# Down projection, every second load: the second part of a weight made by a negated copy and an adding transfer

## The chip, the cores and the metric

The kernel runs on one core of a Trainium2 chip. The core has a matrix engine (TensorE, PE in the profile; its weight loads are a track of their own, PEld), three engines for elementwise work (VectorE, DVE; ScalarE, ACT; GpSimd, POOL), SyncE (SP), which here only issues transfers, and 16 DMA engines that carry every transfer, whichever engine's queue issued it. The engines run side by side and wait for each other through semaphores; each works through its own instructions in order.

The metric is the device time of one execution in microseconds, the median over several runs. The profile is one execution taken with the hardware profiler on, and its times are counted from the start of its span.

## The reference, cut to what matters

A two-layer encoder on 256 tokens of width 1024. Each layer has a token mixer (pooling branch, dilated attention branch, gates, output projection) and then a gated MLP with a width-3 convolution over the tokens. The change lies in the MLP:

```python
a, gval = jnp.split(xn @ w_up, 2, axis=-1)          # w_up: 1024 x 5632
a = lax.conv_general_dilated(a, conv_w[:, None, :], ...) + conv_b
return (jax.nn.gelu(a) * gval) @ w_down             # w_down: 2816 x 1024
...
h = h + _conv_ffn(...)                              # last, a final RMSNorm
```

All inputs and outputs are float32.

## The kernel before, in words

**Numbers in two parts.** TensorE works on a rounded 32-bit format. To keep the precision of float32, an operand is split: the first part is the number rounded to that format, the second is the number less the first part. A product then takes three matmuls: first by first, first by second, second by first. `row_mm` (L582 to L587) does so in the down projection: L585 multiplies the activation's first part with the weight's first part (`wh`), L586 the activation's first part with the weight's second part (`wl`), L587 the activation's second part with `wh`.

**Weights.** `Weights` (L97) feeds all of them. `add` notes a load of 1 MB, which is cut into two pieces of 128x1024 numbers (512 KB); `use` puts the pieces on a list in the order in which TensorE will want them. `load` (L127) issues the transfer from DRAM on SyncE's queue into one of three `raw` buffers. `open_next` (L179) splits a piece: ScalarE casts `raw` into `wh` (L201), and VectorE subtracts `wh` from `raw` into `wl` (L203). There are five buffers for `wh` and five for `wl` (`BUFS`). `get` (L224) hands a piece to the code that multiplies with it, and first sees to it that the three pieces behind it (`LOOK`) are split.

**The MLP.** It goes over 22 blocks f of 128 hidden channels, two at a time (L1331). `up(f)` (L1262) computes a block of the up projection (`proj`, L551; matmuls on L543 with tile `proj_ps`), adds up its sums (L579, L580), does the convolution (L1274 on ScalarE, L1275 and L1278 on VectorE), the GELU (L1288 and L1292 on ScalarE, L1289 and L1293 on VectorE), the gate (L1297 or L1303), and splits the result (L1308, L1309). From f = 6 on, two steps of the down projection follow each pair of blocks. They use the activations of six blocks earlier (`LAG`), and each step multiplies with one piece of `w_down`: four sums (two sets of tokens by two halves of the columns), three matmuls each, tile `res_ps`. The last four pieces are held and multiplied at the end, sum by sum. At f = 4, 8, 12 and 14 half of a group of the gate's values is computed as well (`t_ps`, L667).

The list of pieces is written in the same order ahead of time (L310 to L322): for each second f the columns of `w_up`, then, from f = 6 on, two pieces of `w_down`, and at the end the pieces that are left.

**Order.** The order of each engine's instructions is made when the program is built, by a scheduler that goes by the order in which the code issues them and by its own estimate of when each is ready. It may move an instruction past others of its engine; at run time nothing is reordered.

Of the kernel before, what the change touches and what calls it, by code (L numbers as in the profile page):

```python
# [13 lines left out]
ALU = mybir.AluOpType  # L14
# [82 lines left out]
class Weights:  # L97
# [8 lines left out]
    def __init__(self, tc, pool, idle):  # L106
        self.tc, self.nc, self.pool, self.idle = tc, tc.nc, pool, idle
        self.loads, self.pieces = [], []
        self.n_loaded, self.n_split, self.n_got = 0, 0, 0
        self.raw, self.split = {}, {}  # L110
        self.live = set()
        self.behind, self.later = (), []
        self.last = [None, None]
        self.loads_behind = {}
        self.n_scaled, self.gains = 0, None

    def add(self, src, shape, cuts, tag=None):

        n = len(self.loads)
        self.loads.append((src, shape, tag))  # L120
        return [(n, cut, c_shape) for cut, c_shape in cuts]
# [57 lines left out]
    def open_next(self):  # L179


        nc, i = self.nc, self.n_split
        n, cut, shape, slot = self.pieces[i]
        if slot is None:
            self.live.add(i)
            h, l = (
                self.pool.tile([P, *shape], F32R, tag=tag, bufs=self.BUFS, name=f"{tag}{i}")
                for tag in ("wh", "wl")
            )
        else:  # L190
            tag, part, of = (*slot, 0, 1)[:3]
            if part == 0:
                self.shared = self.idle.tile([P, of, 2, *shape], F32R, tag=tag, name=f"{tag}{i}")
            h, l = self.shared[:, part, 0], self.shared[:, part, 1]
        src = cut(self.raw[n])
        self.split[i] = (h, l)
        self.n_split += 1
        if i >= self.n_scaled:
            def make(n):
                if n == 0:  # L200
                    inst = nc.scalar.copy(out=h, in_=src)  # L201
                else:
                    inst = nc.vector.tensor_sub(out=l, in0=src, in1=h.bitcast(F32))  # L203
                self.last[n] = inst
                return inst

            return [(lambda: make(0), lambda: make(1))]

        def scaled(j):
            k = (i * shape[0] + j) % KD  # L210
            g = self.gains[:, k : k + 1]
            return (
                lambda: nc.scalar.activation(h[:, j], src[:, j], AF.Copy, scale=g),
                lambda: nc.vector.scalar_tensor_tensor(
                    out=l[:, j], in0=src[:, j], scalar=g, in1=h[:, j].bitcast(F32),
                    op0=ALU.mult, op1=ALU.subtract,
                ),

                lambda: nc.vector.tensor_scalar_mul(h[:, j], src[:, j], g),
            )  # L220

        return [scaled(j) for j in range(shape[0])]
# [19 lines left out]
def encoder(ctx, tc, x, w_in, w_pool, pool_scale, w_a, w_b, w_o, norm1, norm2, w_up, conv_w,  # L242
            conv_b, w_down, rel_bias, norm_f, onehot, edges, out):
    nc = tc.nc
# [9 lines left out]
    W = Weights(tc, wpool, big)  # L254

    def cols(w, c0):

        src = w[:, c0 : c0 + 256].rearrange("(k p) c -> p k c", p=P)
        return W.add(
            src, (8, 256), [((lambda t, j=j: t[:, :, j * P : (j + 1) * P]), (8, P)) for j in (0, 1)]  # L260
        )

    def rows(w, r0, n=2, c0=0, width=1024, tag=None, pieces=2):

        src = w[r0 : r0 + n * P, c0 : c0 + width].rearrange("(k p) c -> p k c", p=P)
        h = n // pieces
        return W.add(
            src, (n, width), [((lambda t, j=j: t[:, j * h : (j + 1) * h, :]), (h, width)) for j in range(pieces)],
            tag,
        )  # L270

    first_up = []
    for l in range(DEPTH):
        for g in range(NG):
            c0 = C_V + g * 512
            slots = (("m2", 0, 2), ("m2", 1, 2), ("ybig",), ("at2",)) if g == 0 else ()
            for j in range(2):
                tag = "k1" if l == 0 and g == 1 and j == 0 else None
                W.use(rows(w_in[l], j * 512, 4, c0, 512, tag), slots[2 * j : 2 * j + 2])
        if l == 0:  # L280
            W.n_scaled = len(W.pieces)
        for c in range(3, -1, -1):
            W.use(cols(w_in[l], c * 256))
        for n, c in enumerate(PAIRS):
            pool = ([], [])
            if n == 1:
                pool = W.add(
                    w_pool[l].rearrange("g (k p) c -> p (g k) c", p=P), (8, 256),
                    [((lambda t, j=j: t[:, 4 * j : 4 * j + 4, :]), (4, 256)) for j in range(2)],
                )  # L290
                pool = (pool[:1], pool[1:])
            W.use(pool[0] + cols(w_in[l], C_Q + c * 256))
            W.use(pool[1] + cols(w_in[l], C_K + c * 256))
        for w, c0 in ((w_a[l], 0), (w_in[l], C_GP)):
            for c in (c0, c0 + 512):
                W.use(rows(w, 0, 4, c, 512) + rows(w, 512, 4, c, 512))
        for c in (0, 512):
            W.use(rows(w_in[l], 0, 4, C_GA + c, 512) + rows(w_in[l], 512, 4, C_GA + c, 512))
            W.use(rows(w_b[l], 0, 4, c, 512))
        for c in range(4):  # L300
            W.use(rows(w_o[l], c * 256))
        first_up.append((len(W.pieces), len(W.loads)))
        slots = (("v1",), ("ybig",), ("at2",))
        for j in range(2):
            tag = None if j else "k1"
            W.use(rows(w_up[l], j * 512, 4, 0, 512, tag), slots[2 * j : 2 * j + 2])
        for n in range(3):
            for j in range(2):
                W.use(rows(w_up[l], j * 512, 4, DFF + n * 512, 512))
        for f in range(4, NF, 2):  # L310
            if f in HALF_GROUPS:
                n, j = HALF_GROUPS[f]
                W.use(rows(w_up[l], j * 512, 4, DFF + n * 512, 512))
            a = cols(w_up[l], f * P)
            if f >= 4 * NQ:
                g = cols(w_up[l], DFF + f * P)
                a = [a[0], g[0], a[1], g[1]]
            W.use(a)
            if f >= LAG:
                W.use(rows(w_down[l], (f - LAG) * P))  # L320
        for f in range(NF - LAG, NF, 2):
            W.use(rows(w_down[l], f * P))  # L322
# [228 lines left out]
    def proj(x2, n=1):  # L551


        if not ready:
            pieces = [W.get() for _ in range(n)]
            ps = [mmp.tile([P, 2, S], F32, tag="mm", name="proj_ps") for _ in range(n)]
            two_sums(
                x2, KD,
                *(
                    (b, lambda k, wh=wh: wh[:, k, :], lambda k, wl=wl: wl[:, k, :])  # L560
                    for b, (_, (wh, wl)) in zip(ps, pieces)
                ),
            )
            for i, _ in pieces:
                W.free(i)
            ready.extend((b[:, 0], b[:, 1]) for b in ps)
        return ready.pop(0)

    def halves(a):

        return a.rearrange("p (t m) -> p t m", t=2)
# [331 lines left out]
    for l in range(DEPTH):  # L903
# [49 lines left out]
        for gi in range(3, -1, -1):  # L953
# [10 lines left out]
            cur, n = u, S + 2 * PAD  # L964
            sh = 1
            while sh < w:
# [3 lines left out]
                    out=nxt[:, :, 0:n], in0=cur[:, :, 0:n], in1=cur[:, :, sh : sh + n]  # L970
# [7 lines left out]
            if hw > 1:  # L978
# [5 lines left out]
                out=pd, in0=cur[:, :, o : o + S], scalar=1.0 / w, in1=u[:, :, PAD : PAD + S],  # L984
# [130 lines left out]
        for m, c in enumerate(PAIRS):  # L1115
# [7 lines left out]
            for n in range(4):  # L1123
                if m == 1:
                    next(pool_parts)
                src, rest = (halves(a) for a in proj(x2, 1 + (m != 1)))
                hd = 2 * c + n % 2
                scale = HD**-0.5 if n < 2 else 1.0
                if hd < HPG:
# [3 lines left out]
                        out=lo[:, hd], in0=src, scalar=scale, in1=hi[:, hd].bitcast(F32),  # L1133
# [3 lines left out]
                        out=lo[:, hd], in0=rest, scalar=scale, in1=lo[:, hd].bitcast(F32),  # L1137
                        op0=ALU.mult, op1=ALU.add,
                    )
                else:  # L1140
# [3 lines left out]
                        out=o, in0=src, scalar=scale, in1=o, op0=ALU.mult, op1=ALU.add  # L1144
# [18 lines left out]
        for cc in HALVES:  # L1163
# [4 lines left out]
            for t in range(2):  # L1168
                nc.vector.scalar_tensor_tensor(
                    out=pa[:, t, cc], in0=th[:, t], scalar=1.0, in1=pa[:, t, cc],  # L1170
# [4 lines left out]
        piece, load = first_up[l]  # L1175
        made = None
        for n, cc in enumerate(HALVES):
# [5 lines left out]
            for t in range(2):  # L1183

                with tc.issue_after((turned if t else made[1]).ins) if n + t else ExitStack():
                    nc.vector.scalar_tensor_tensor(
                        out=th[:, t], in0=th[:, t], scalar=1.0, in1=ps[t], op0=ALU.add, op1=ALU.mult
# [187 lines left out]
```

## Time and profile before

| | |
|---|---|
| Median of 3 runs | 859.94 us (859.87 to 860.45) |
| Profiled execution, span | 858.0 us |
| TensorE busy | 851.6 us (99%) |
| VectorE busy | 661.2 us (77%) |
| ScalarE busy | 493.8 us (58%) |
| GpSimd busy | 32.0 us (4%) |
| Moved by DMA | 186.81 MB, 218 GB/s on average |

The profiled execution has its span as its only time: from the first to the last instruction of the program. The timed runs also count what lies around the span. A row of the profile names the line of the kernel, the engine, the operation and the tiles (out<-in), the shape and the number of instructions; behind the bar stand the busy time, the mean time of one in nanoseconds, and the idle time of the engine ahead of them with what ended it. A row of the timeline has the start, the time taken, and in square brackets the idle time of the engine ahead of it. Matmuls overlap in TensorE's pipeline: a row of 0.39 us for a 128x512 matmul starts 0.23 us behind the one before.

### The profile page before, as it was taken

To read this page: it belongs to the slowest core of one execution; us is meant where nothing else is said; L and a number is where in the kernel's file an instruction comes from. 1 tells how busy PE (TensorE), PEld (TensorE's weight loads), DVE (VectorE), ACT (ScalarE), POOL (GpSimd) and SP (SyncE) were. 2 spreads that over 40 slices of the span, in tenths; PEclk is the share of its full clock that TensorE was granted. 3 is DMA by queue.
4 is the path that set the end of the run, shared out by engine and by line. 5 is a ranking of instruction groups with operands and counts; after the bars stand their busy time and mean duration, and the time that the engine had idled before them with its cause. 6 is when DMAs were issued, how large, how long until landed. Compare 5 with 4: busy or idle time off the path is not lost.

```text
span 858.0 us, 11823 instructions
## 1 busy us (share of the span) xinstructions
PE 851.6 (99%) x4343; PEld 727.9 (85%) x4343; DVE 661.2 (77%) x1050; ACT 493.8 (58%) x795; POOL 32.0 (4%) x98
## 2 busy tenths in 40 slices
PE   9999999999999999999999999999999999999997
PEld 8888888888888888888888889988888888888886
DVE  7998796667767788888855987874776777988894
ACT  7756654455445476666645665543654555775672
POOL 1710000000010000000000000000000000000001
PEclk9999999999999999999999999999999999999999
DMA  9686547766747876666736555658667478676641
GB/s 331 217 248 206 196 163 231 240 228 229 250 182 246 270 249 231 231 235 206 245 99 209 184 199 192 198 175 268 226 243 275 154 249 259 246 256 208 239 147 49
DMA packets 136387, 186.81 MB, mean 218 GB/s; under 512 B 5561, under 2 KB 88193, under 8 KB 136329
## 3 DMA queue, kind: packets, MB, share of 16 engines
q1 hardware_dynamic: 136168, 185.79, 63.8%
q8 instruction: 34, 0.56, 0.3%
q10 hardware_dynamic: 160, 0.27, 0.1%
q14 instruction: 25, 0.20, 0.1%
HBM read 172.39 MB, written 13.65 MB: 217 GB/s over the span
## 4 chain that ended last, share of the span: by engine, by line
PE 99%; DVE 0%; ACT 0%; POOL 0%; issue 0%; POOLq 0%; ACTq 0%
PE proj_ps L543 34%; PE t_ps L667 30%; PE v_ps L667 6%; PE res_ps L586 6%; PE res_ps L585 6%; PE res_ps L587 6%; PE v_ps L895 3%; PE v_ps L802 1%; PE pool_ps L543 1%; PE o_ps L1086 1%; PE s_ps L1034 1%; PE s_ps L1029 1%; PE o_ps L1082 1%; PE xt_ps L481 1%; PE gain_ps L372 0%; PE xt_ps L750 0%
## 5 line engine op out<-in xcount | busy, mean ns | idle before, releaser
L203 DVE TENSOR_TENSOR wl<-raw,wh 128x1024 fp32r<-128x1024 f32 x274 | 329.8, 1217 | 88.1 <-ACT wh L201 73.6
L201 ACT CAST wh<-raw 128x1024 fp32r<-128x1024 f32 x274 | 284.3, 1049 | 118.3 <-PE t_ps L667 49.0
L543 PE MATMUL proj_ps<-x,wh 128*128 128x512 f32 x832 | 196.9, 390 | 0.0
L543 PEld LDWEIGHTS proj_ps<-x,wh 128*128 128x128 f32 x832 | 154.3, 188 | 30.9
L667 PE MATMUL t_ps<-wh,x 128*128 128x512 f32 x576 | 179.7, 390 | 0.0
L667 PEld LDWEIGHTS t_ps<-wh,x 128*128 128x128 f32 x576 | 107.8, 188 | 22.3
L667 PE MATMUL t_ps<-wl,x 128*128 128x512 f32 x288 | 112.1, 389 | 0.0
L543 PEld LDWEIGHTS proj_ps<-x,wl 128*128 128x128 f32 x832 | 105.4, 191 | 3.0
L543 PE MATMUL proj_ps<-x,wl 128*128 128x256 f32 x832 | 107.8, 283 | 0.0
L586 PE MATMUL res_ps<-wl,actq 128*128 128x512 f32 (+1 forms) x184 | 70.0, 380 | 0.0
L587 PE MATMUL res_ps<-wh,actk 128*128 128x512 f32 (+1 forms) x184 | 69.9, 380 | 0.0
L585 PE MATMUL res_ps<-wh,actq 128*128 128x512 f32 (+1 forms) x184 | 69.7, 381 | 0.0
L667 PEld LDWEIGHTS t_ps<-wl,x 128*128 128x128 f32 x288 | 54.1, 188 | 11.2
L667 PE MATMUL t_ps<-wh,po 128*128 128x512 f32 x128 | 41.4, 395 | 0.0
L587 PEld LDWEIGHTS res_ps<-wh,actk 128*128 128x128 f32 x184 | 34.6, 188 | 6.6
L586 PEld LDWEIGHTS res_ps<-wl,actq 128*128 128x128 f32 x184 | 34.6, 188 | 6.4
L585 PEld LDWEIGHTS res_ps<-wh,actq 128*128 128x128 f32 x184 | 34.5, 188 | 6.3
L454 POOL TENSOR_SCALAR ss<-ss 128x1 f32<-128x1 f32 x8 | 2.0, 253 | 779.6 <-ACT junk L447 779.6
L1308 ACT CAST actq<-g 128x256 fp32r<-128x256 f32 x44 | 17.0, 403 | 20.7 <-DVE g L1297 20.0
L667 PEld LDWEIGHTS t_ps<-wh,po 128*128 128x128 f32 x128 | 24.0, 188 | 4.9
L447 ACT ACTIVATE junk<-h 128x512 f32<-128x512 f32 (+1 forms) x19 | 10.5, 553 | 28.6 <-DVE h L445 28.5
L579 ACT COPY a<-proj_ps 128x256 f32<-128x256 f32 x36 | 13.6, 389 | 23.3 <-PE proj_ps L543 23.3
(204 smaller groups left out, 1148.9 us busy)
## 6 DMA issues: line engine op xcount, KB each, us to landing
raw<-in_w_in_dram SPq DMA_DIRECT2D x58, 1024.0 KB, 5.4
raw<-in_w_up_dram SPq DMA_DIRECT2D x44, 1024.0 KB, 6.9
raw<-in_w_down_dram SPq DMA_DIRECT2D x22, 1024.0 KB, 4.7
raw<-in_w_a_dram SPq DMA_DIRECT2D x8, 1024.0 KB
raw<-in_w_o_dram SPq DMA_DIRECT2D x8, 1024.0 KB, 7.1
crossing<-crossing SPq DMA_DIRECT2D x12, 512.0 KB, 5.4
turning<-turning SPq DMA_DIRECT2D x8, 512.0 KB, 2.8
turned_p<-turning SPq DMA_DIRECT2D x32, 128.0 KB, 3.3
```

The costliest lines, as they stand in the source:

```text
L201: inst = nc.scalar.copy(out=h, in_=src)
L203: inst = nc.vector.tensor_sub(out=l, in0=src, in1=h.bitcast(F32))
L447: nc.scalar.activation(junk[:, 0 : cc.stop - cc.start], h[:, t, cc], AF.Square, scale=D**-0.5, accum_out=ss[:, n : n + 1],)
L481: nc.tensor.transpose(pt[:, k, :], xn[:, c0 : c0 + P], ident)
L543: nc.tensor.matmul(out, w(k), x, start=(steps is first and k == 0), stop=(steps is last and k == nk - 1), skip_group_check=turns["rest"],)
L579: nc.scalar.copy(out=out, in_=sums[1])
L585: nc.tensor.matmul(ps, ah, wh, start=first, stop=False, skip_group_check=on)
L586: nc.tensor.matmul(ps, ah, wl, start=False, stop=False, skip_group_check=on)
L587: nc.tensor.matmul(ps, al, wh, start=False, stop=last, skip_group_check=on)
L667: nc.tensor.matmul(ps, x2[:, 2 * n + j, part, t, :], w[:, j, :], start=(n + m == 0), stop=(n == last and m == 5),)
L895: nc.tensor.matmul(ps[t], a[:, k, t, :], w[:, j, :], start=(k + m == 0), stop=(k == KD - 1 and m == 2),)
L1308: nc.scalar.copy(out=ah, in_=g)
```

## The change

At f = 6, 10, 14 and 18 the two pieces of `w_down` put on the list are marked (`by_dma`). For a marked piece the second part is made in another way. ScalarE still casts `raw` into `wh`. Then ScalarE writes minus `raw` into `wl`, which is rounded on the way, so that `wl` holds minus the first part. Then a transfer on GpSimd's queue reads the same rows of `w_down` from DRAM a second time and adds them onto `wl`, which leaves the weight less its first part. VectorE's subtraction falls away for these pieces. The loads at the other f, and the six pieces behind f = 20, are as before.

```diff
@@ class Weights, __init__
         self.n_scaled, self.gains = 0, None
+        self.by_dma = set()
@@ class Weights, open_next
-        src = cut(self.raw[n])
+        load, src = n, cut(self.raw[n])
...
             def make(n):
                 if n == 0:
                     inst = nc.scalar.copy(out=h, in_=src)
+                elif i in self.by_dma:
+                    nc.scalar.mul(out=l, in_=src, mul=-1.0)
+                    nc.gpsimd.dma_start(out=l, in_=cut(self.loads[load][0]), accum_op=ALU.add)
+                    return None
                 else:
                     inst = nc.vector.tensor_sub(out=l, in0=src, in1=h.bitcast(F32))
@@ encoder, the list of pieces
             if f >= LAG:
+                if f % 4 == 2:
+                    W.by_dma |= {len(W.pieces), len(W.pieces) + 1}
                 W.use(rows(w_down[l], (f - LAG) * P))
```

`self.loads[load][0]` is the part of `w_down` in DRAM from which the raw buffer was loaded, and `cut` takes the piece's half of it.

## The prediction

> **What bounds the kernel now.** I read the page first, then the busy time by stretches, then the rows of ScalarE and TensorE around the loads that the change names.
>
> ```profile
> span 858.0 us, 11823 instructions
> PE 851.6 (99%) x4343; PEld 727.9 (85%) x4343; DVE 661.2 (77%) x1050; ACT 493.8 (58%) x795; POOL 32.0 (4%) x98
> ```
>
> The span is 858.0 us, and the median of the three runs is 859.94: 1.9 us lie around the span, and I add every difference to 859.94. TensorE is busy for all but 6.4 us. The chain of waits agrees (PE 99%), so a microsecond counts only where TensorE waits for it. The change works in the gated MLP; the first stretch below lies in that of the first layer, the second in that of the second, and the last holds the end. Busy time of each engine by stretch (stretch and its length, then PE, PEld, DVE, ACT, POOL, the granted clock, the DMA share, GB/s):
>
> ```profile
> 300.00:360.00 60.00, 60.00 (x304) 51.24 (x303) 51.30 (x91) 40.37 (x71) 0.00 (x0) 1.00 0.70 237
> 720.00:780.00 60.00, 60.00 (x304) 51.24 (x303) 50.92 (x87) 40.60 (x70) 0.00 (x0) 1.00 0.70 242
> 820.00:858.00 38.00, 32.31 (x169) 27.68 (x167) 24.40 (x44) 18.20 (x37) 2.16 (x7) 0.96 0.27 101
> ```
>
> In the MLP TensorE has no idle time at all, VectorE is at 85% and ScalarE at 67%. Of the 6.4 us in which TensorE is idle, 5.7 lie in the last stretch (38.00 less 32.31), behind the last matmul, which the change does not touch. So relieving VectorE can gain nothing here; the question is only whether TensorE now has to wait.
>
> **The change, part by part.** It concerns pieces of w_down, 128x1024 each. The loads at f = 6, 10, 14 and 18 of each layer are changed: 4 loads, 8 pieces a layer, 16 in all. VectorE's subtraction goes, ScalarE gets a second pass, and GpSimd's queue gets a transfer that adds 512 KB from DRAM onto the piece.
>
> ```profile
> L203 DVE TENSOR_TENSOR wl<-raw,wh 128x1024 fp32r<-128x1024 f32 x274 | 329.8, 1217 | 88.1 <-ACT wh L201 73.6
> L201 ACT CAST wh<-raw 128x1024 fp32r<-128x1024 f32 x274 | 284.3, 1049 | 118.3 <-PE t_ps L667 49.0
> ```
>
> VectorE loses 16 x 1.217 = 19.5 us, worth nothing in time by the stretches above. ScalarE gains 16 negated copies; I price one at the 1.05 us of the cast of the same shape, 16.8 us in all. Even if all eight of a layer fell into the 60 us shown, ScalarE would go from 40.4 to 48.8 of 60, still covered by a TensorE that is the slower one. If that cover were gone, 16.8 us would be the price. VectorE and ScalarE still have to finish each f's activation only six f later (LAG), so a microsecond of delay there reaches nobody.
>
> The copy holds the raw buffer in place of the subtraction. By the rows below it ends 0.8 us later than the subtraction did for the first pair (306.25 against 305.46) and for the second a microsecond earlier, so SyncE's next load moves by about that, nothing to a load that goes out several pieces ahead. On GpSimd's queue the transfers stand between the statistics of the two normalizations, and GpSimd does nothing in the MLP's stretches (0.00): nothing is queued behind them until the down projection ends. SyncE's queue gets no new instruction.
>
> The step that matters is the new chain. Before: cast, subtraction, TensorE. After: cast, negated copy, issue on GpSimd, transfer, TensorE. I take the lead of a piece to be the time from the end of its negated copy to the first matmul that reads its second part (res_ps<-wl, L586), and call L the time from the end of that copy to the landing. TensorE loses L minus the lead, where that is positive.
>
> First pair (f = 6), first layer; the built program puts the copies behind the first cast and behind the two L1274 activations:
>
> ```profile
> 299.29 1.05 ACT L201 CAST wh<-raw 128x1024 fp32r<-128x1024 f32 x1 [2.04 <-DMA raw<-in_w_down_dram]
> 301.92 0.39 ACT L579 COPY a<-proj_ps 128x256 f32<-128x256 f32 x1 [1.58 <-PE proj_ps L543]
> 303.16 1.05 ACT L201 CAST wh<-raw 128x1024 fp32r<-128x1024 f32 x1
> 304.11 1.09 ACT L1274 ACTIVATE y<-a,prm 128x256 f32<-128x256 f32 x2
> 304.24 1.22 DVE L203 TENSOR_TENSOR wl<-raw,wh 128x1024 fp32r<-128x1024 f32 x1 [0.51 <-ACT wh L201]
> 303.15 0.39 PE L586 MATMUL res_ps<-wl,actq 128*128 128x512 f32 x1
> 308.94 0.39 PE L587 MATMUL res_ps<-wh,actk 128*128 128x512 f32 x1
> 311.21 0.39 PE L586 MATMUL res_ps<-wl,actq 128*128 128x512 f32 x1
> ```
>
> The first copy fits into the 1.58 us that ScalarE was idle, and ends near 300.34 + 1.05 = 301.4. TensorE read this second part at 303.15, but the built program now puts the piece's four first-part matmuls and the next up projection ahead of it, so it is wanted near 309.2 (one matmul behind the row at 308.94, where it went on with this piece before): lead 7.8. The second copy ends at 304.11 + 1.09 + 1.05 = 306.25; its reader is the row at 311.21: lead 5.0. Moving matmuls within TensorE's order costs nothing: the same number, and each loads its own weights either way.
>
> Second pair (f = 10), both copies behind L1274:
>
> ```profile
> 328.63 1.09 ACT L1274 ACTIVATE y<-a,prm 128x256 f32<-128x256 f32 x2
> 335.94 0.39 PE L586 MATMUL res_ps<-wl,actq 128*128 128x512 f32 x1
> 338.66 0.39 PE L586 MATMUL res_ps<-wl,actq 128*128 128x512 f32 x1
> ```
>
> The copies end at 330.77 and 331.82: leads 5.2 and 6.8. Third pair (f = 14), behind the two L1292, and fourth (f = 18), the first behind its cast, the second behind L1292:
>
> ```profile
> 358.76 0.72 ACT L1292 ACTIVATE y<-y 128x256 f32<-128x256 f32 x2
> 368.83 0.39 PE L586 MATMUL res_ps<-wl,actq 128*128 128x512 f32 x1
> 382.01 1.98 ACT L201 CAST wh<-raw 128x1024 fp32r<-128x1024 f32 x2
> 386.21 0.72 ACT L1292 ACTIVATE y<-y 128x256 f32<-128x256 f32 x2
> 390.85 0.39 PE L586 MATMUL res_ps<-wl,actq 128*128 128x512 f32 x1
> 393.57 0.39 PE L586 MATMUL res_ps<-wl,actq 128*128 128x512 f32 x1
> ```
>
> Third: 359.47 + 1.05 = 360.5, lead 8.3 for the first piece, some 10 for the second. Fourth: the first cast ends at 383.05, the copy at 384.1, lead 6.7; L1288, the second cast and L1292 follow, and the second copy ends near 387.7 (1.05 behind a L1292 that ends at about 386.7 now): lead 5.9. A wait for one piece of a pair shifts TensorE for the other too, so each pair costs L minus its smaller lead: 5.0, 5.2, 8.3, 5.9. The second layer has the same order and repeats them.
>
> L is not in this trace: no transfer adds, and none is issued from GpSimd. Bounds, from issue to landing of SyncE's transfers (KB each, median us):
>
> ```profile
> raw<-in_w_up_dram SPq DMA_DIRECT2D x44, 1024.0 KB, 6.9
> raw<-in_w_down_dram SPq DMA_DIRECT2D x22, 1024.0 KB, 4.7
> turning<-turning SPq DMA_DIRECT2D x8, 512.0 KB, 2.8
> DMA to landing us min/median/max: 4.7/5.0/9.1
> ```
>
> From below: 512 KB that cost no more than a plain transfer, 2.8 us. From above: the slowest weight load, 9.1, with a microsecond for the issue as my estimate (SyncE's own issue rows are 0.37 us), 10. To add, the transfer has to fetch its destination as well as its source, so 1024 KB are read: the 1024 KB rows are the nearest. Of those I take w_up's 6.9, because it runs in the same stage beside the other loads, as these transfers will. L = 7.
>
> Sum: 2 x ((7 - 5.0) + (7 - 5.2) + 0 + (7 - 5.9)) = 2 x 4.9 = 9.8 us, so 859.9 + 9.8 = 869.7.
>
> Two rules bear on L. The Trainium skill (DMA: Bandwidth & Descriptors, section "Anatomy of one DMA — SWDGE (gpsimd) path") gives a transfer from GpSimd's queue about 2 us plus its bytes at 436 GB/s: 3.2 us for 512 KB by estimate. It also says (Collectives: The Full Stack, "The bandwidth ceiling: the fold count and why AG ≠ RS ≠ AR") that an adding transfer is slowed by its two source reads and not by the add: 1.2 us more, 4.4. By both, no lead is exceeded and the sum is 859.9. No run here shows either yet; the loads of this trace, at 4.7 to 6.9 us, are slower than the first rule's 4.4 for 1024 KB.
>
> **The rivals.** One ends on the other side: the transfer lands within the smallest lead, L under 5.0, and TensorE never waits: 859.9. For it: 4.7 us for 1024 KB of w_down and 2.8 for 512 KB. Against it: L contains GpSimd's issue as well, and the DMA engines are at 0.70 in this stage, so most transfers meet a load. This is also where the two rules above end. It decides at L = 5.4, where the stalls are 2 x (0.4 + 0.2) = 1.2 us.
>
> A second rival: the adding transfers are slow, L of 10 and above. For it: the 9.1 in the row above, and a path that no row shows. Against it: two thirds of the loads need half of that. At 10 the sum is 2 x (5.0 + 4.8 + 1.7 + 4.1) = 31.2, 891; each further microsecond adds 8. TensorE would then stand still for about 5 us six times over, and its clock may drop: it does so at the end, where it goes idle (0.96 for the last 38 us). The Trainium skill (TensorE: Matmul & The Clock Gate, "Why this matters for your kernels") names idle gaps over some 3 us as what halves the clock; at L = 7 no gap is that long.
>
> A third: the transfers take the DMA engines from the weight loads, and first parts come late. They add 16 x 1 MB of reads to 186 MB, about a tenth in these stages, and ScalarE waited for w_up and w_down only four times (us in all, times, longest):
>
> ```profile
> ACT wh L201 <- DMA raw<-in_w_up_dram: 7.8, 2, 4.3
> ACT wh L201 <- DMA raw<-in_w_down_dram: 3.2, 2, 2.0
> ```
>
> If each of the eight pairs held one load up by 2 us beyond its slack, that would be 16 us, 876: inside the range.
>
> Faster than before would need idle time of TensorE in these stages, and there is none.
>
> **How the numbers follow.** Forecast, L from 5.4 to 9.5: chance 0.60, its own range 861 to 887 (at 9.5: 2 x (4.5 + 4.3 + 1.2 + 3.6) = 27.2), of which the third rival is 0.06. Landing in time: 0.24. Slow landing: 0.12. Faster for a reason I do not see: 0.04. Change within 0.2% (1.7 us) is about what a measurement of this kernel can tell from none. So faster 0.04, same 0.24, slower 0.72. The range has to take in the second case and leaves out the slow landing: 859.2 to 887.
>
> **What would show it.** TensorE's rows on L586 should for the first time have idle time ahead of them that ends with the transfer, at f = 6, 10 and 18 of both layers, about 2, 1.8 and 1.1 us, none at f = 14. The transfer's median from issue to landing should be near 7. ScalarE's busy time should be 16.8 up, VectorE's 19.5 down, the DMA share up by a few hundredths. A landing under 5 us or TensorE waits of 4 and more would make it wrong; so would waits that end with a cast.

## The result and the profile after

The changed kernel takes 896.3 us (median; 893.0 to 898.2) against 860.2 for the kernel before beside it: a ratio of 1.0416, interval 1.0398 to 1.0433. It is slower by 36 us, more than the 9.8 of the prediction and outside its range. The profiled execution took 893.0 us, with a span of 891.2; its lines answer to those of 858.0. Added lines shift the numbers: L586 is L593 now, L587 is L594, L585 is L592, L201 is L202, and L203 is L208; the negated copy is L204, the transfer L205.

From the page of the changed kernel: busy time, the granted clock in 40 slices, the queue of the new transfers, and the groups of the rows that matter:

```profile
span 891.2 us, 11865 instructions
...
PE 862.4 (97%) x4343; PEld 733.6 (82%) x4343; DVE 645.1 (72%) x1034; ACT 508.4 (57%) x811; POOL 45.5 (5%) x114
...
PEclk9999999999999999999999999999999999989989
...
q0 software_dynamic: 2304, 8.39, 5.0%
...
L593 PE MATMUL res_ps<-wl,actq 128*128 128x512 f32 (+1 forms) x184 | 74.1, 403 | 22.0 <-DMA wl<-in_w_down_dram 22.0
...
L205 POOL DMA_DIRECT2D wl<-in_w_down_dram x16 | 14.2, 885 | 285.1 <-ACT wl L204 162.4 <-DVE g L1304 68.1 <-ACT y L1295 54.3
```

From the view of the groups by line, VectorE's subtraction and ScalarE's negated copy:

```profile
L208 DVE TENSOR_TENSOR wl<-raw,wh 128x1024 fp32r<-128x1024 f32 x258 | 311.0, 1219 | 102.5 <-ACT wh L202 87.2 <-PE proj_ps L550 14.4
...
L204 ACT ACTIVATE wl<-raw 128x1024 fp32r<-128x1024 f32 x16 | 16.4, 1048 | 0.0
```

These two are what was priced: VectorE 18.8 us less (329.8 to 311.0), ScalarE 16.4 us more. TensorE does the same 4343 matmuls, but is busy for 862.4 us instead of 851.6 and has gained 22.0 us of idle time, all of it on L593 and all of it ended by the new transfer. 10.8 + 22.0 = 32.8, of 33.2 us by which the span has grown. So two things are to be explained: why it waits for 22.0 us, and why the same matmuls take 10.8 us longer.

The waits first, in TensorE's timeline (start, time taken, and the idle time ahead in brackets): four of the first layer, three of the second.

```profile
315.06 0.50 PE L593 MATMUL res_ps<-wl,actq 128*128 128x512 f32 x1 [3.46 <-DMA wl<-in_w_down_dram]
343.93 0.79 PE L593 MATMUL res_ps<-wl,actq 128*128 128x512 f32 x1 [3.84 <-DMA wl<-in_w_down_dram]
403.70 0.50 PE L593 MATMUL res_ps<-wl,actq 128*128 128x512 f32 x1 [2.99 <-DMA wl<-in_w_down_dram]
407.91 0.50 PE L593 MATMUL res_ps<-wl,actq 128*128 128x512 f32 x1 [1.20 <-DMA wl<-in_w_down_dram]
752.22 0.50 PE L593 MATMUL res_ps<-wl,actq 128*128 128x512 f32 x1 [3.31 <-DMA wl<-in_w_down_dram]
782.75 0.80 PE L593 MATMUL res_ps<-wl,actq 128*128 128x512 f32 x1 [3.87 <-DMA wl<-in_w_down_dram]
846.50 0.79 PE L593 MATMUL res_ps<-wl,actq 128*128 128x512 f32 x1 [3.33 <-DMA wl<-in_w_down_dram]
```

They stand at f = 6, f = 10 and f = 18 (there both pieces wait in the first layer), and then at the same three places of the second layer. At f = 14 there is none. The transfers land later than the 7 us that the prediction took from the end of the copy. From issue to landing, by the rows of L205:

```profile
DMA to landing us min/median/max: 6.0/8.5/12.0
```

The copy's end lies 0.3 us ahead of the issue by the timeline of ScalarE and GpSimd, so L is about 8.8 at the median, and from 6.3 to 12.3 over the 16.

Most of the 10.8 us are the clock. Busy time of each engine by stretch (columns as in the prediction; PE first, the granted clock third from the end):

```profile
313.22:316.63 3.41, 1.57 (x7) 1.31 (x8) 2.63 (x5) 1.56 (x3) 0.00 (x0) 1.00 1.03 347
316.63:320.04 3.41, 3.41 (x17) 2.83 (x16) 3.14 (x5) 3.36 (x7) 0.00 (x0) 1.00 1.05 386
...
750.12:753.53 3.41, 1.31 (x6) 1.10 (x7) 3.12 (x7) 1.74 (x3) 0.00 (x0) 1.00 1.04 329
753.53:756.95 3.42, 3.42 (x10) 2.65 (x9) 2.95 (x4) 2.70 (x5) 0.00 (x0) 0.50 1.05 391
777.43:780.84 3.41, 1.45 (x7) 0.88 (x5) 2.89 (x6) 3.33 (x7) 0.00 (x0) 1.00 0.98 237
780.84:784.25 3.41, 1.50 (x4) 1.21 (x5) 3.40 (x6) 1.28 (x2) 0.00 (x0) 0.50 1.05 280
784.25:787.67 3.42, 3.42 (x10) 2.65 (x9) 0.00 (x0) 0.00 (x0) 0.00 (x0) 0.50 1.03 363
787.67:791.08 3.41, 3.41 (x17) 2.79 (x16) 1.84 (x3) 2.16 (x4) 0.00 (x0) 1.00 0.17 64
```

After the wait that ended at 752.22 a stretch of 3.41 us has half the clock, after the one at 782.75 two of them: ten matmuls fit in where seventeen fit at full clock. The trace has four such periods ahead of the end, of 3.41 us at 343.9 and 753.5 and of 6.83 us at 780.8 and 845.7: 20.5 us at half speed. TensorE is busy for 17.8 of them by the same view, so 8.9 us are lost to the clock. The other 1.9 us of busy time need no clock: the half-columns kernel below, which waits at full clock, is busy for 853.8 us, 2.2 more than the kernel before. The kernel before has no half clock until its tail.

### The profile page after: what moved, and what is told of

Its sections match the earlier page's. It is cut to its first block, busy times and chain, and to the rows that moved or that the text cites. A ratio compares the mean times of both kernels' runs of the same rounds, so it can differ in the third digit from the quotient of the medians.

```text
span 891.2 us, 11865 instructions
## 1 busy us (share of the span) xinstructions
PE 862.4 (97%) x4343; PEld 733.6 (82%) x4343; DVE 645.1 (72%) x1034; ACT 508.4 (57%) x811; POOL 45.5 (5%) x114
## 4 chain that ended last, share of the span: by engine, by line
PE 86%; DMA 8%; ACT 3%; issue 2%; DVE 1%; SPq 0%; POOLq 0%; POOL 0%; ACTq 0%
PE t_ps L674 29%; PE proj_ps L550 27%; PE v_ps L674 6%; DMA wl<-in_w_down_dram 6%; PE res_ps L593 5%; PE res_ps L594 5%; PE res_ps L592 5%; PE v_ps L902 2%; DMA raw<-in_w_up_dram 1%; PE v_ps L809 1%; PE pool_ps L550 1%; ACT wh L202 1%; DMA crossing<-crossing 1%; PE o_ps L1093 1%; PE s_ps L1041 1%
## 5 line engine op out<-in xcount | busy, mean ns | idle before, releaser
L208 DVE TENSOR_TENSOR wl<-raw,wh 128x1024 fp32r<-128x1024 f32 x258 | 311.0, 1219 | 102.5 <-ACT wh L202 87.2
L202 ACT CAST wh<-raw 128x1024 fp32r<-128x1024 f32 x274 | 284.8, 1049 | 151.7 <-PE t_ps L674 51.7
L593 PE MATMUL res_ps<-wl,actq 128*128 128x512 f32 (+1 forms) x184 | 74.1, 403 | 22.0 <-DMA wl<-in_w_down_dram 22.0
L594 PE MATMUL res_ps<-wh,actk 128*128 128x512 f32 (+1 forms) x184 | 72.9, 396 | 0.0
L592 PE MATMUL res_ps<-wh,actq 128*128 128x512 f32 (+1 forms) x184 | 71.5, 394 | 0.0
L593 PEld LDWEIGHTS res_ps<-wl,actq 128*128 128x128 f32 x184 | 36.3, 197 | 32.0 <-DMA wl<-in_w_down_dram 25.3
L594 PEld LDWEIGHTS res_ps<-wh,actk 128*128 128x128 f32 x184 | 36.5, 198 | 7.0
L592 PEld LDWEIGHTS res_ps<-wh,actq 128*128 128x128 f32 x184 | 36.0, 197 | 7.0
L1316 DVE TENSOR_TENSOR actk<-g,actq 128x256 fp32r<-128x256 f32 x44 | 17.7, 421 | 15.7 <-ACT actq L1315 14.3
L205 POOL DMA_DIRECT2D wl<-in_w_down_dram x16 | 14.2, 885 | 285.1 <-ACT wl L204 162.4
L1296 DVE SCALAR_TENSOR_TENSOR y<-y,y 128x256 f32<-128x256 f32 x44 | 17.7, 421 | 13.7 <-ACT y L1295 13.6
```

The lines of the kernel that those rows point to most:

```text
L205: nc.gpsimd.dma_start(out=l, in_=cut(self.loads[load][0]), accum_op=ALU.add)
L592: nc.tensor.matmul(ps, ah, wh, start=first, stop=False, skip_group_check=on)
L593: nc.tensor.matmul(ps, ah, wl, start=False, stop=False, skip_group_check=on)
L594: nc.tensor.matmul(ps, al, wh, start=False, stop=last, skip_group_check=on)
L1296: nc.vector.scalar_tensor_tensor(out=y2, in0=y2, scalar=1.0, in1=y, op0=ALU.add, op1=ALU.mult)
L1316: nc.vector.tensor_sub(out=al, in0=g, in1=ah.bitcast(F32))
```

## The experiments

**ScalarE's pass alone.** VectorE subtracts as before, but ScalarE still writes its negated copy first.

```diff
                     nc.scalar.mul(out=l, in_=src, mul=-1.0)
-                    nc.gpsimd.dma_start(out=l, in_=cut(self.loads[load][0]), accum_op=ALU.add)
-                    return None
+                    inst = nc.vector.tensor_sub(out=l, in0=src, in1=h.bitcast(F32))
```

> ScalarE's second pass alone: it writes the negated copy into wl for the same 16 pieces, and VectorE's subtraction then overwrites it; no transfer. Theory A (all of the loss is TensorE waiting for the 16 transfers, and the half clock behind those waits): no wait, 860 +- 1. Rival B (the extra 16.8 us of ScalarE delay other work): 865 to 877.

Measured: 860.2 us, ratio 0.9997 (0.9988 to 1.0007). ScalarE's 16 copies cost nothing, and neither does holding the raw buffer for them. This is read from the time alone. What costs has to come from the transfer.

**The transfers alone, one place.** Only f = 14 is changed, the pair for which the prediction had worked out the largest leads, 8.3 and some 10.

```diff
-                if f % 4 == 2:
+                if f == 14:
```

> Only the load at f = 14 is changed, 4 pieces instead of 16; its leads are 8.3 and 10 us, and its landings in the changed kernel 6.1 to 9.1. Theory A: 860 to 862. Rivals B and B2 (a cost for each piece): a quarter of the loss, about 869.

Measured: 860.8 us, ratio 1.0013 (1.0003 to 1.0022). The landing, from the rows of its L205:

```profile
DMA to landing us min/median/max: 5.8/8.1/10.1
```

and from TensorE's waits:

```profile
PE res_ps L593 <- DMA wl<-in_w_down_dram: 0.2, 1, 0.2
```

The four transfers are as slow as the others (8.1 against 8.5), and TensorE waits once, for 0.16 us. So the length of a transfer does not decide alone: with a lead of 8 to 10 us it is hidden.

**The transfers with nobody waiting for them.** The copy and the adding transfer go to a spare tile that is never read; VectorE subtracts as before.

```diff
-                    nc.scalar.mul(out=l, in_=src, mul=-1.0)
-                    nc.gpsimd.dma_start(out=l, in_=cut(self.loads[load][0]), accum_op=ALU.add)
-                    return None
+                    part = i - min(self.by_dma & {i - 1, i})
+                    if part == 0:
+                        self.spare = self.idle.tile([P, 2, *shape], F32R, tag="m2", name=f"spare{i}")
+                    s = self.spare[:, part]
+                    nc.scalar.mul(out=s, in_=src, mul=-1.0)
+                    nc.gpsimd.dma_start(out=s, in_=cut(self.loads[load][0]), accum_op=ALU.add)
+                    inst = nc.vector.tensor_sub(out=l, in0=src, in1=h.bitcast(F32))
```

> The 16 negated copies and the 16 adding transfers stay, but go into a spare tile that nobody reads; VectorE makes wl as before. Theory A: 860 to 862, TensorE never waits; the transfers take 6 to 12 us as in the changed kernel. Rival B2 (the transfers take the DMA engines from the weight loads): 868 or more, with waits for raw.

Measured: 868.4 us, ratio 1.0098 (1.0067 to 1.0129), between what the theories expected. TensorE's waits:

```profile
PE t_ps L678 <- ACT wh L202: 4.1, 3, 1.9
PE t_ps L678 <- DVE wl L212: 1.6, 3, 0.5
```

ScalarE's waits:

```profile
ACT wh L202 <- DMA raw<-in_w_up_dram: 22.6, 8, 6.9
```

the longest of these in ScalarE's timeline:

```profile
344.78 1.04 ACT L202 CAST wh<-raw 128x1024 fp32r<-128x1024 f32 x1 [6.94 <-DMA raw<-in_w_up_dram]
```

and the landing of the weight loads on SyncE's queue, by the rows of L138 (in every run the trace has the landing of 16 of the 146 loads of 1 MB, the same ones):

```profile
DMA to landing us min/median/max: 4.6/5.5/12.3
```

ScalarE waits 22.6 us for loads of `w_up` (7.8 before). The load that lands 12.3 us after its issue is one of `w_down` that goes out beside the transfers of f = 10 in the second layer; the same load took 5.9 us before. (The 9.1 of the kernel before is another load, the first 1 MB load of the program.) And TensorE is held at three places by a cast and the subtraction behind it, with the clock halved once behind it (6.83 us at 346.5). So the adding transfers do harm beyond their own landing: they hold up the loads beside them. In the changed kernel that same load takes 12.4 us, and ScalarE waits for `w_up` more than before as well:

```profile
ACT wh L202 <- DMA raw<-in_w_up_dram: 17.4, 8, 4.2
```

No wait of TensorE ends with a cast there; it would fit that the loads catch up while it waits for the second parts, but no run shows that. At three places SyncE's issue of the next `w_down` load also took 2.6 to 4.6 us instead of 0.37, and once 2.9 in the kernel with zeros below; why is not settled.

**The same with a plain copy.** The spare-tile kernel without the adding.

```diff
-                    nc.gpsimd.dma_start(out=s, in_=cut(self.loads[load][0]), accum_op=ALU.add)
+                    nc.gpsimd.dma_start(out=s, in_=cut(self.loads[load][0]))
```

> The spare-tile kernel with a plain copy from DRAM in place of the adding transfer; VectorE still subtracts, nobody reads the spare tile, the output is whole. The spare-tile kernel cost 8 us: its weight loads took up to 12.3 us to land (9.1 before) and TensorE then waited for casts and subtractions. Theory A: that delay is the extra reads and the slow packets of the adding transfers, which a plain copy about halves: 860 to 863, slowest weight load near 9 to 10 us, TensorE waits under 2 us in all. Theory B: it is the place of the transfers in the stage (the queue, the moment at which they go out), whatever they do: 866 to 870, slowest load again near 12, waits of about 7 us.

Measured: 860.6 us, ratio 1.0004 (0.9994 to 1.0014). TensorE waits for no piece at all. The queue, from its page:

```profile
q0 software_dynamic: 2304, 8.39, 2.9%
```

ScalarE's waits:

```profile
ACT wh L202 <- DMA raw<-in_w_up_dram: 8.8, 5, 3.2
```

and the landing of the weight loads:

```profile
DMA to landing us min/median/max: 4.8/5.1/9.5
```

The same bytes are written at the same places from the same queue, and what costs time is gone: ScalarE waits for `w_up` about as long as before (8.8 against 7.8), and TensorE not at all. So it is the adding that costs the 8 us. The loads are not quite as before, though: the `w_down` load that took 5.9 us before and 12.3 beside adding transfers takes 8.8 beside plain copies. The 9.5 is again the first 1 MB load of the program. The queue's share is 2.9% of 16 engines' span against 5.0% in the changed kernel: per packet of 4 KB (2048 of them; the other 256 are of 4 bytes) 0.029 x 858.7 x 16 / 2048 = 0.19 us against 0.35.

**A plain copy in the place of the adding transfer.** As the changed kernel, but the transfer overwrites `wl`.

```diff
-                    nc.gpsimd.dma_start(out=l, in_=cut(self.loads[load][0]), accum_op=ALU.add)
+                    nc.gpsimd.dma_start(out=l, in_=cut(self.loads[load][0]))
```

> The 16 transfers copy w_down over wl instead of adding to it (wl then holds the whole weight: this kernel leaves out the subtraction for these pieces); same queue, same bytes written, the destination is not read. Theory C1 (the second read makes L): packets near 160 ns instead of 327, landing about 2.6 us earlier by the packets and more where it shares the engines, 5 to 7 us, TensorE waits under 5 us in all, 862 to 868. Rival C2 (GpSimd's issue and the fixed part make L): landing 7.5 to 8.5 and 885 or more.

Measured: 874.9 us, ratio 1.0170 (1.0115 to 1.0225). The landing, by the rows of L205:

```profile
DMA to landing us min/median/max: 4.5/6.6/8.5
```

and TensorE's waits:

```profile
PE res_ps L593 <- DMA wl<-in_w_down_dram: 10.7, 6, 2.7
```

The landing falls from 8.5 to 6.6 us, the waits from 22.0 to 10.7, the half-clock periods from 20.5 to 6.8. The landing is what theory C1 expected, but the time and the waits are over its 868 and its 5 us, because a landing of 6.6 still misses most leads. Adding thus accounts for about 21 of the 36 us; the two executions behind this time lie at 871.7 and 878.1, so the share is good to some 3 us. The other 15 or so are the detour itself: even a plain transfer, with L at 6.6 + 0.3 = 6.9, misses leads of 5.0, 5.2 and 5.9. The prediction's sum with 6.9 gives 2 x (1.9 + 1.7 + 0 + 1.0) = 9.2 us of waits, against 10.7. Whether a plain transfer from SyncE's queue would land earlier was not tried.

**Half of the columns.** The transfer adds onto columns 0 to 511, VectorE subtracts the others.

```diff
-                    nc.scalar.mul(out=l, in_=src, mul=-1.0)
-                    nc.gpsimd.dma_start(out=l, in_=cut(self.loads[load][0]), accum_op=ALU.add)
+                    c = slice(0, 512)
+                    nc.scalar.mul(out=l[:, :, c], in_=src[:, :, c], mul=-1.0)
+                    nc.gpsimd.dma_start(
+                        out=l[:, :, c], in_=cut(self.loads[load][0])[:, :, c], accum_op=ALU.add
+                    )
+                    c = slice(512, D)
+                    nc.vector.tensor_sub(out=l[:, :, c], in0=src[:, :, c], in1=h[:, :, c].bitcast(F32))
                     return None
```

> Only the first 512 columns of the 16 pieces go by copy and adding transfer (256 KB), VectorE subtracts the others. If L is by bytes (8 packets of 4 KB for each engine, 2.6 us without a rival load, twice that with one): packets of half the time, landing 1.3 to 3 us earlier, 5.5 to 7; waits 5 to 10 us in all, 865 to 872. If L is fixed cost and the loads queued ahead: landing as before, 885 or more.

Measured: 872.3 us, ratio 1.0140 (1.0106 to 1.0174), from two executions at 870.7 and 873.9: the upper end of what was expected if L goes by bytes. The queue, from its page:

```profile
q0 software_dynamic: 2304, 4.20, 2.8%
```

the landing:

```profile
DMA to landing us min/median/max: 4.9/6.7/9.5
```

and TensorE's waits:

```profile
PE res_ps L598 <- DMA wl<-in_w_down_dram: 8.2, 6, 2.0
```

Half the bytes by adding take the queue what all of them took by copying (2.8% and 2.9%), and land as late (6.7 and 6.6). So an adding packet of 2 KB takes about as long as a plain one of 4 KB. A straight line through the two sizes puts 8.5 - 2 x (8.5 - 6.7) = 4.9 us of the landing at what would not shrink with the bytes, as an estimate. No wait is over 2.0 us, and the clock stays full until the tail.

**Longer leads.** For the changed pieces TensorE does all matmuls that read `wh` first, so that the first one on `wl` comes seven matmuls, 1.6 us, later.

```diff
+                if i in W.by_dma:
+                    four = [(ps[t][c], t, slice(c * 512, c * 512 + 512)) for t in range(2) for c in range(2)]
+                    for x, w in ((ah, wh), (al, wh), (ah, wl)):
+                        for p, t, cc in four:
+                            nc.tensor.matmul(p, x[:, t], w[:, 0, cc], start=(k == 0 and x is ah and w is wh), stop=False)
+                    W.free(i)
+                    yield
+                    continue
                 for t in range(2):
                     for c in range(2):
                         one(
```

> For the 16 pieces the eight matmuls with the first part come ahead of the four with the second: the second part is wanted 7 x 0.227 = 1.6 us later. Theory A: the seven waits of 3.46, 3.84, 2.99, 1.20, 3.31, 3.87 and 3.33 us shrink by 1.6 each to 11.2 in all, none over 3 us, and the clock stays whole: 871 to 874. If the lost clock goes with the sum of the waits and not with their length: 876 to 880. If the waits are for something else: 896.

Measured: 885.4 us, ratio 1.0287 (1.0264 to 1.0310); 871 to 874 was expected. TensorE's waits:

```profile
PE res_ps L618 <- DMA wl<-in_w_down_dram: 15.7, 8, 3.0
```

the last of them in its timeline:

```profile
842.88 1.65 PE L618 MATMUL res_ps<-wl,actq 128*128 128x512 f32 x3 [2.20 <-DMA wl<-in_w_down_dram]
```

and two stretches, the one in which it waits and the next:

```profile
839.29:842.70 3.41, 1.39 (x7) 0.81 (x5) 3.41 (x7) 1.60 (x3) 0.00 (x0) 1.00 0.99 231
842.70:846.12 3.42, 3.24 (x8) 2.60 (x9) 1.07 (x1) 1.31 (x3) 0.00 (x0) 0.50 0.97 313
```

The waits fall by 6.3 us, less than six times 1.6, while the landing has grown to a median of 9.1. What the expectation had wrong is the clock: 17.1 us still ran at half of it, once behind a wait of only 2.20.

**The clock by itself.** In three pieces of each layer (the second at f = 6, the first at f = 10, the second at f = 18) TensorE gets 15 matmuls with zeros (3.4 us) ahead of the first matmul on `wl`, so that it works instead of standing still.

```diff
+            if n == NF and k in (1, 4, 13):
+                nc.tensor.matmul(ps[0][0], ah[:, 0], wh[:, 0, 0:512], start=False, stop=False)
+                for _ in range(15):
+                    nc.tensor.matmul(ps[0][0], ah[:, 0], zeros, start=False, stop=False)
+                nc.tensor.matmul(ps[0][0], ah[:, 0], wl[:, 0, 0:512], start=False, stop=False)
...
```

> Ahead of the first matmul with the second part, in the six pieces where TensorE waited over 2.9 us, 15 matmuls with a tile of zeros into the same sum (3.4 us of work that changes nothing). If the half clock follows from idle time: the waits become busy, no half clock, 10 us less than the changed kernel and the waits nearly the same, 882 to 887. If the clock drops for another reason: 893 to 898 as before.

Measured: 885.8 us, ratio 1.0290 (1.0268 to 1.0312).

From its page:

```profile
span 885.5 us, 12041 instructions
...
PE 874.0 (99%) x4433; PEld 744.4 (84%) x4433; DVE 646.3 (73%) x1035; ACT 509.4 (58%) x811; POOL 46.4 (5%) x114
...
PEclk9999999999999999999999999999999999999999
```

90 matmuls more, and the kernel is 10.5 us faster than the changed one, with the clock full until its tail. At f = 18 of the first layer the zeros stand one piece too late: the wait of 2.99 us was at the first piece, and there TensorE still waits 1.75 us, in a stretch of 3.41 us with 1.66 of work and without a half clock behind it. The waits that are left come to 3.3 us, so zeros and waits together (90 x 0.227 + 3.3 = 23.7) fill about the time that the waits took before. So about 10 us of the 36 are the half clock, near the 8.9 counted above.

## Why the prediction was wrong

**What held.** TensorE is the bound, the relief of VectorE gained nothing, and ScalarE's 16 copies are hidden: ScalarE's pass alone left the time as it was. Nothing waits behind the transfers on GpSimd's queue. The direction was right, and so was the place: waits on L593 that end with the transfer at f = 6, 10 and 18 of both layers, none at f = 14. The leads can be checked together: put L = 8.8 into the prediction's own sum and it gives 2 x (3.8 + 3.6 + 0.5 + 2.9) = 21.6 us of waits, where the trace has 22.0. One by one, from the end of the copy to the start of the wait, they were 5.2 at f = 6 (5.0 forecast) and 5.4 at f = 10 (5.2) in both layers; at f = 18 the first piece had 5.1 in the first layer (6.7 forecast) and the second 6.2 in the second (5.9). As L ranges from 6.3 to 12.3, it is partly luck that the sum comes so close.

**The step that failed first: L = 7.** It was taken from the `w_up` row, as the nearest for 1024 KB of reads; it measures 8.8 at the median, and up to 12.3. That row is weaker than it looks: of its 44 loads the trace has the landing of two, at 4.8 and 8.9 us, and 6.9 is the middle between them. The 9.1 that bounded L from above is the first 1 MB load of the program, 5.8 us after its start and far from this stage. This term was 9.8 us and should have been 22. The reasoning that two reads make 512 KB like 1024 KB was right in kind, as the plain copy shows: without the adding 1.9 us of the landing go. And L = 7 is nearly what a plain copy takes on this path (6.9). What the row of SyncE's loads could not carry was the rest of the path, the issue on GpSimd (0.87 us) and the wait behind the loads that are queued at that moment. In the trace's packets the first packet of a pair's first transfer comes 2.0 to 2.4 us after the issue begins at f = 6, 14 and 18, and 3.7 to 3.9 at f = 10, where two weight loads went out some 3 us before. The pair's second transfer starts 4.1 to 6.7 us after its issue; how much of that is the first one and how much the weight loads is open.

The two rules of the Trainium skill gave 3.2 us (DMA: Bandwidth & Descriptors, "Anatomy of one DMA — SWDGE (gpsimd) path") and, with the two reads, 4.4. The fastest of the 16 transfers took 6.0, and even the plain copies took 4.5 to 8.5 in the place of the adding transfers and 3.5 to 8.6 into the spare tile, so in this stage, beside the weight loads, both figures are too low. The rule that an adding transfer is slowed by its two reads (Collectives: The Full Stack, "The bandwidth ceiling: the fold count and why AG ≠ RS ≠ AR") agrees in kind: 0.35 us for a packet against 0.19.

**The step that failed second: the clock.** Half clock stood only in the slow-landing rival, at waits of about 5 us; at L = 7 it was left out because no gap was that long. In the changed kernel it cost some 9 us, behind four waits of 3.3 to 3.9; with longer leads a wait of 2.2 was enough. With it the upper end of the range, worked out for L = 9.5 as 27.2 us of waits alone, would have been up to some 10 us higher.

Together: 9.8 forecast + 12.2 for L + 10.8 for the longer busy time, most of it the clock, = 32.8, beside 33.2 of span and 892.7 of time. The profiled execution took 893.0. That the median lies 3.3 us above it is not explained by a trace. It fits a clock that works in fixed stretches, in which the same waits fall otherwise in each execution, but that is only argued.

**The rivals.** Landing in time fell with the shortest transfer: 6.0 us and never under the smallest lead. The slow landing was right that the clock would drop. Its total of 891 is near only by luck: its L of 10 was too long at the median, and its 31 us of waits, without a term for the clock, came out as 22 of waits and 11 of longer busy time. The argument against it, that two thirds of the loads need half of 10 us, is not in the rows: of the 16 loads whose landing the trace of the kernel before has, nine land within 5.5 us. The third, loads held up by the transfers, is real: it is the 8 us of the spare-tile kernel, and plain copies do not cost them. In the changed kernel no wait of TensorE ends with a first part that came late, but the held-up loads may have shortened one lead: at f = 18 of the first layer ScalarE waited 3.22 us for `w_up`, where it did not wait before, and the copy behind that is the one whose lead came out at 5.1 instead of 6.7.

No version is faster than the kernel before. TensorE has nothing to gain in these stages, and the best forms (f = 14 alone, or copies that nobody reads) end level with it or 0.1% above.

## What to carry to other kernels

Before work is moved from an engine to a transfer, work out for each place how long it has between the last input and the first reader, and leave the place alone where that is under the landing of a transfer of the same kind, measured in the same stage: here 8.5 us for 512 KB, and up to 12. Price a wait of TensorE at more than its length, because four of the six waits of 3.0 to 3.9 us were followed by 3.4 or 6.8 us at half clock. And an adding transfer also slows the loads that share the DMA engines with it, so a place with enough lead of its own can still cost time next door.

## What the runs showed of the hardware

**The clock goes by fixed stretches.** All half-clock periods of a run start at whole multiples of 3.413 us from each other (343.93 and 753.53: 120 of them) and, ahead of the tail, last one or two. In the rows above, a full-clock stretch with TensorE busy for 1.57 us was followed by full clock, and those with 1.45, 1.39 and 1.31 by half. The nearest one on the other side is in the spare-tile kernel:

```profile
343.10:346.52 3.42, 1.56 (x7) 0.71 (x5) 0.67 (x1) 1.74 (x4) 0.00 (x0) 1.00 1.06 407
346.52:349.93 3.41, 2.88 (x8) 2.22 (x8) 3.41 (x7) 3.28 (x5) 0.00 (x0) 0.50 0.20 80
```

Worked out in the same way for all full-clock stretches with waits in six of the kernels (the changed one, the spare tile with adding, the plain copy in the place of the adding transfer, half of the columns, longer leads, and zeros), every one with 1.56 us or less was followed by half clock, and every one with 1.57 or more by full. The ends of matmuls are modelled, so the boundary is near 1.6 us and no finer. So the 3.46 us wait at 315.06, which two stretches share, cost no clock, and one of 2.20 us that lay mostly in one stretch did. Once halved, the clock came back after one stretch where TensorE was idle for under 0.2 us in it, and only after a second one where it was idle for over 0.5. The Trainium skill (TensorE: Matmul & The Clock Gate, "What's actually happening") describes a free-running window of 3413 ns, which agrees. Its advice in "Why this matters for your kernels" that idle gaps over some 3 us halve the clock does not agree: 2.20 us were enough, and 3.46 were not always.

**Adding costs at the issue too.** An adding transfer took GpSimd 0.885 us to issue, a plain one of the same shape 0.557:

```profile
L205 POOL DMA_DIRECT2D wl<-in_w_down_dram x16 | 8.9, 557 | 278.8 <-ACT wl L204 184.9 <-DVE g L1304 60.2 <-ACT y L1295 32.9
```

This row is from the kernel with the plain copy in the place of the adding transfer; the one of the changed kernel stands in the section on the result.
